# Conditioning loads of the last projection tiles moved to GpSimd's queue, value weights split ahead of the query rotation, five buffers for split queries and keys

## The chip, the core and the metric

The kernel runs on one core of a Trainium2 chip. The metric is the device time of one execution in microseconds; less is better. TensorE multiplies, VectorE (DVE) and ScalarE (ACT) work element by element, GpSimd (POOL) does some of that and starts transfers, and SyncE (SP) starts transfers only. ScalarE starts transfers too. Each engine takes its instructions in program order, and waits for others by semaphores.

## The reference

One encoder block on a sequence of 1024 positions with 1024 channels, all in float32:

```
ada = silu(c) @ w_ada + b_ada;  sh1, sc1, gt1, sh2, sc2, gt2 = split(ada, 6)
h = rms(x, g_pre_mix) * (1 + sc1) + sh1
q_lat, kv_lat, k_rope_raw, u, gate_cols = split(h @ w_in)       # 384, 256, 32, 512, 2048
branch_a = attention(rms(q_lat) @ w_uq, rms(kv_lat) @ w_uk, rms(kv_lat) @ w_uv, rotated parts) @ w_o
branch_b = a * sigmoid(g), where a, g = split(gelu(s5(u)) @ w_glu)   # s5: a state-space scan, both directions
mixed = (sigmoid(gate_a) * branch_a + sigmoid(gate_b) * branch_b) @ w_mix
x = x + gt1 * rms(mixed);  h = rms(x, g_pre_ffn) * (1 + sc2) + sh2
x = x + gt2 * rms((silu(h @ w_g) * (h @ w_up)) @ w_out)
```

`w_ada` is a 1024 x 6144 matrix that meets a single vector, so the conditioning is 48 column blocks of 128, each a row-wise dot product.

## The kernel before, in words

Channels lie on the partitions, positions in the free dimension, in two halves of 512. Every large product is done three times in a reduced format on split operands (high times high, high times low, low times high): `mm3`, lines 199 to 203. Weights come through `WStream` (line 150): SyncE loads a raw tile (two buffers), ScalarE casts its high part, VectorE subtracts the low part (three buffers of each). `get(ahead)` hands out a tile and splits as many as `ahead` beyond it, one by default; the loads of later raw tiles follow. The order of the list is: 26 tiles of `w_in`, three of `w_uq`, `w_uk`, `w_uv`, eight of `w_glu`, then the rest.

The stage around the change:

- **Projection tiles 10 to 25** (loop at line 950). `proj_tile` multiplies 48 large matmuls (two halves of eight blocks of three); between the halves and after them one step of the state-space part (until tile 22) and one step of a latent's norm is put in. ScalarE evacuates each half.
- **Norms of the latents** (`q_norm`, `kv_stats`, from tile 20 and 22): squares on ScalarE, their additions on VectorE (`lat_stats`, line 846), one-column sums on TensorE (line 245), a root in small VectorE steps, two diagonal tiles on VectorE, and `lat_apply` (line 862) spreads them by a matmul with ones (line 871), then scales and splits the latents.
- **Conditioning blocks 16 to 47** (`ada_load`, line 923, `ada_load2`, line 942, `ada_do`, line 933). A block of 512 KB, or two halves of 256 KB in buffers that the state-space part used (`er`, `ei`, `mr`, `mi`, `tz`, `r`), is multiplied by silu(c) and summed by VectorE. Two are loaded at tile 18, two each at tiles 20 to 22, four each at tiles 23 and 24, one in each gated-unit tile (`glu`, line 1118), and eight in the feed-forward part. At tile i the statements are: flush, `ada_do` (all live blocks), the next loads, a norm step. A load given to `later` goes on a list; `flush` starts all that is on it from ScalarE's queue:

```
    def later(dst, src):
        pending.append((dst, src))

    def flush(keep=0):
        while len(pending) > keep:
            A_.dma_start(*pending.pop(0))
```

- **Queries, keys, values.** Four tiles of the position-free queries (`uq_nope`, 18 large matmuls each), with the key and value latents' scaling between them; `uq_rope` (36 matmuls, then the rotation on VectorE out of four PSUM buffers, with the first Gelus of `y_chain` on ScalarE between its halves); then `uk_half` and `uv_tiles` by turns, six matmuls each, eight of both. `split_store` (line 1011) splits a query or key half in two and stores both parts to HBM by SyncE; its tiles are in the pool `sg`. PSUM has four buffers named `mm` and four named `s`; `uv_tiles` and every second half use `s`.
- Then eight gated-unit tiles, attention, the mixing product and the feed-forward part.

Of the kernel before, what the change touches and what calls it, by code (L numbers as in the profile page):

```python
# [33 lines left out]
KEEP0, ADA0, ADAN = 2, 18, 2  # L34
# [5 lines left out]
GLU_ADA, ATT_ADA = (1,) * NJ, (2,)  # L40
# [17 lines left out]
class Ops:  # L58
# [6 lines left out]
    def tt(self, o, a, b, op):  # L65
        return self.eng.tensor_tensor(o, a, b, op=op)  # L66
# [24 lines left out]
def _body(tc, a, out):  # L91
    nc = tc.nc
    V, A_, PE, G, SY = nc.vector, nc.scalar, nc.tensor, nc.gpsimd, nc.sync
# [6 lines left out]
    def pool(name, bufs=1, space=None, side=None, stack=None):  # L100
        kw = {}
        if space is not None:
            kw["space"] = space
        if side is not None:
            kw["side"] = side
        return (stack or es).enter_context(tc.tile_pool(name=name, bufs=bufs, **kw))
# [35 lines left out]
# [6 lines that stand above are left out]
# [153 lines left out]
    for kind, i, hs in units:  # L301
        if kind == "in":
            wl += [(a["wfi"][2 * i], KD * P), (a["wfi"][2 * i + 1], KD * P)]
        elif i < last or hs == (0,):
            c = 2 * FGROUPS[i] * P
            wl += [(a["wfo"][m, :, 2 * starts[i] * P:2 * starts[i] * P + c], c) for m in range(KD // 2)]
    win = WStream(wp, wl, D, (2, 3))
# [285 lines left out]
    nr = pool("nr", bufs=2, stack=q_es)  # L593
# [217 lines left out]
    def norm_step():  # L811
        for g in norms:
            next(g, None)

    def proj_tile(i, done):
        w = win.get()
        pss = []
        for h in range(2):
            ps = ps_mm()
            c = slice(h * HF, (h + 1) * HF)  # L820
            for k in range(KD):
                mm3(ps, w, hhi[k][:, c], hlo[k][:, c], k, k == 0, k == KD - 1)
            pss.append(ps)
            if i > 3:
                if h == 0:
                    s5_next()
                    norm_step()
        done(pss)
        if i > 3:
            s5_next()  # L830

    for i in range(4, 10):
        def done(ps, i=i):
            for h in range(2):
                t = ev.tile([P, HF], F32, name="ev", tag="ev")
                A_.copy(t, ps[h])
                A_.dma_start(pdram[i - 4, :, h * HF:(h + 1) * HF], t)
# [70 lines left out]
    def q_norm():  # L908
        raw = [load_rows(0), load_rows(1), load_halves(2, ("u", "u"), 3)]
        yield  # L910
        rc = yield from lat_stats(raw, lambda i: s5_half(f"t{i}"), ps_s5)
        yield from lat_apply(raw, rc, g_q, qhi, qlo, lambda i: s5_half(f"t{i}"), ps_s5)

    def kv_stats():
        raw = [load_halves(3 + i, (f"g{i}", f"g{i}"), 2) for i in range(2)]
        yield
        kv_rc.append((yield from lat_stats(raw, lambda i: s5_half(("vr", "vi", "z0")[i]), ps_s5)))
# [3 lines left out]
    ada_rest = list(range(16, 48))  # L921

    def ada_load(n, pl, tag, bufs=None, eng=G):
        for _ in range(min(n, len(ada_rest))):
            i = ada_rest.pop(0)
            t = pl.tile([P, D], F32, name=tag, tag=tag, bufs=bufs)
            if eng is None:
                later(t, a["wada"][i])
            else:
                eng.dma_start(t, a["wada"][i])  # L930
            ada_live.append((t, i))

    def ada_do(n=8):
        while ada_live and n:
            t, i = ada_live.pop(0)
            if isinstance(t, list):
                ada_reduce2(t, i)
            else:
                ada_reduce(None, t, i)
            n -= 1  # L940

    def ada_load2(tags):

        i = ada_rest.pop(0)
        t = [s5b.tile([P, 512], F32, name=n, tag=n, bufs=tags[2]) for n in tags[:2]]
        for x, c in zip(t, halves):
            later(x, a["wada"][i][:, c])
        ada_live.append((t, i))

    for i in range(10, 26):  # L950
        def done(ps, i=i):
            for h in range(2):
                t = ev.tile([P, HF], F32, name="ev", tag="ev")
                A_.activation(t, ps[h], AF.Sigmoid)
                A_.dma_start(gdram[i - 10, :, h * HF:(h + 1) * HF], t)
        proj_tile(i, done)
        flush()
        if ADA0 <= i < QN0:
            ada_do()
            if i < QN0 - 1:  # L960
                ada_load(ADAN, nr, "nr", None, None)
        if i >= QN0:
            ada_do()
            for tags, first in ADA_TAGS:
                if first <= i < 25:
                    ada_load2(tags)
            if i == QN0:
                norms.append(q_norm())
            if i == KN0:
                norms.append(kv_stats())  # L970
            norm_step()
# [12 lines left out]
    r_es = ExitStack()  # L984
# [4 lines left out]
    gp = pool("gp", bufs=2, side="right", stack=gp_es)  # L989
    yp = pool("y", side="right", stack=y_es)  # L990
    kvp = pool("kv", stack=r_es)
    rp = pool("rp", stack=r_es)
    sg = pool("sg", bufs=3, stack=r_es)
    csb = [rp.tile([P, S], F32, name=f"cs{i}") for i in range(2)]
    G.memset(vhi[:, :, :, 64:66].bitcast(F32), 1.0)
    G.memset(vlo[:, :, :, 64:66].bitcast(F32), 0.0)
# [69 lines left out]

    def uq_rope():

        w = win.get()
        pss = [dense_tile(w, i, 3, qhi, qlo) for i in range(2)]  # L1070
        qr = [qkd["qr"][e].rearrange("(h a r) s -> a h r s", a=2, r=16) for e in range(2)]
        yield
        prev = []
        for h, c in enumerate(halves):
            for i, op in enumerate((ALU.subtract, ALU.add)):
                ti = rp.tile([P, HF], F32, name="qra", tag="qra", bufs=3)
                u = rp.tile([P, HF], F32, name="qrb", tag="qrb")
                tt(ti, pss[i][h], csb[0][:, c], ALU.mult)
                tt(u, pss[1 - i][h], csb[1][:, c], ALU.mult)
                tt(ti, ti, u, op)  # L1080
                prev.append((ti, SCALE, [qr[e][i][:, :, c] for e in range(2)]))
                if len(prev) > 1:
                    split_store(*prev.pop(0))
            yield
        for p in prev:
            split_store(*p)
# [26 lines left out]
    def gb_load(m):  # L1113
        if m < KD:
            gbs[m] = gp.tile([P, S], F32, name="gb", tag="gb")
            later(gbs[m], gdram[m])

    def glu(m):

        w = win.get()  # L1120
        pa = dense_tile(w, 0, 4, yhi, ylo)
        pg = dense_tile(w, 1, 4, yhi, ylo)
        ada_do()
        ada_load(min(GLU_ADA[m], len(ada_rest) - 8), gp, "wada", 3, G if m else None)
        flush()
        gb = gbs.pop(m)
        sgm = gp.tile([P, S], F32, name="sgm", tag="sgm")
        for h, c in enumerate(halves):
            A_.activation(sgm[:, c], pg[h], AF.Sigmoid)
            tt(sgm[:, c], pa[h], sgm[:, c], ALU.mult)  # L1130
            tt(sgm[:, c], sgm[:, c], gb[:, c], ALU.mult)
        later(mbd[m], sgm)
        gb_load(m + 2)
# [3 lines left out]
    for i in range(4):  # L1137
        if i % 2 == 0:
            w = win.get()
# [13 lines left out]
    w = win.get()  # L1153
# [165 lines left out]
    for i in range(len(steps) + LAG):  # L1319
        if 0 <= i < len(steps):  # L1320
            h, kt = steps[i]
            if kt == 0 and h + 2 < NH:
                load_qk(h + 2)
            pt = scores(h, kt)
        j = i + LEAD
        if NJ <= j < len(steps):
            mh_, mt = steps[j]
            ps = mx_ps()
            max_tile(mh_, mt, [ps[:, c] for c in halves])
            V.reduce_max(mcol[mh_][:, mt:mt + 1], ps, axis=mybir.AxisListType.X)  # L1330
        if 0 <= i < len(steps):
            ptiles[i] = p_low(*pt)
        if NJ <= j < len(steps) and mt == NJ - 1:
            max_row(mh_)
        if i in ATT_ADA:
            ada_do(1)
            ada_load(min(1, len(ada_rest) - 8), gp, "wada", 3)
        if i == NJ:
            gp_es.close()
            op = pool("o", side="right", stack=o_es)  # L1340
            ohi += [op.tile([P, S], F32R, name=f"ohi{k}") for k in range(4)]
            olo += [op.tile([P, S], F32R, name=f"olo{k}") for k in range(4)]
        if NB <= i < len(steps):
            st = (i - NB) % (2 * NJ)
            if st == 0 and i >= 2 * NJ:
                norm_b(h // 2 - 1)
            if NC <= st < NC + 4 and i >= 2 * NJ:
                norm_c((i - NB) // (2 * NJ) - 1, st - NC)
        if i in (20, 28):
            win.split()  # L1350
            win.load()
        if i >= LAG:
            pv(*steps[i - LAG], ptiles.pop(i - LAG))
# [21 lines left out]
    with ExitStack() as m_es:  # L1375
# [39 lines left out]
        w = [win.get(), win.get()]  # L1415
# [5 lines left out]
        for m in range(KD):  # L1421
            if m >= 4 and m % 2 == 0:
                w = [win.get()]
# [238 lines left out]
    for u, (kind, i, hs) in enumerate(units):  # L1662
# [14 lines left out]
        if i < last:  # L1677
            for m in range(KD):
                if m % 2 == 0:
                    w = win.get()  # L1680
# [132 lines left out]
```

## Time and profile before

| | us |
|---|---|
| three runs | 1737.35, 1736.61, 1736.26 |
| median | 1736.61 |
| profiled execution | 1737.2 |
| its span, first to last instruction | 1735.4 |

| engine | busy us | share of the span |
|---|---|---|
| TensorE, matmuls | 1639.5 | 94% |
| TensorE, weight loads (beside the matmuls) | 1325.3 | 76% |
| VectorE | 976.7 | 56% |
| ScalarE | 553.1 | 32% |
| GpSimd | 147.9 | 9% |

The mean granted clock of TensorE is 0.968 of full speed. Starting transfers is not counted as busy. A queue of ScalarE or SyncE is written ACTq or SPq. A wait is put down to what came last before the waiting instruction began. Most vector helpers are recorded on lines 66 and 74, all large matmuls on lines 201 to 203, so the names of the tiles tell them apart: `mm` and `s` are PSUM, `whi` and `wlo` split weights, `sghi` and `sglo` split queries and keys, `er<-in_wada` a half of a conditioning block.

### The profile page before, as it was taken

The numbers are of one execution on the slowest core, as the hardware profiler recorded it, in microseconds if no ns is written. First come the engines' busy times: TensorE is split into PE (matmuls) and PEld (weight loads), VectorE is DVE, ScalarE is ACT, GpSimd is POOL, SyncE is SP. The second block draws the span as 40 slices with busy tenths as digits, with TensorE's granted clock in tenths as the row PEclk, the third lists the DMA queues.
The fourth block names the chain that finished last, engine by engine and source line by source line (L and its number), as shares of the span: only waits on it lengthen the run. The fifth ranks groups of instructions, "written<-read, shape, count | busy, mean of one in ns | idle before, by whom it ended". The sixth has DMA issues, their size and how long they took to land.

```text
span 1735.4 us, 19440 instructions
## 1 busy us (share of the span) xinstructions
PE 1639.5 (94%) x7486; PEld 1325.3 (76%) x7486; DVE 976.7 (56%) x1613; ACT 553.1 (32%) x743; POOL 147.9 (9%) x191
## 2 busy tenths in 40 slices
PE   7989999986869999999999999999999999999995
PEld 7868887875648867776777777888888888888875
DVE  4978898844574777885455565222322322323367
ACT  3242312222252147767233344321111121111243
POOL 0340000000031000000233220000000000000002
PEclk9899999987889999999999999999999999999998
DMA  6342333452878541420443252212211111111234
GB/s 260 121 119 96 111 102 96 132 171 93 277 233 265 153 126 34 98 44 13 153 133 128 79 200 94 99 58 72 71 55 52 61 38 48 60 32 46 83 119 148
DMA packets 92540, 189.67 MB, mean 109 GB/s; under 512 B 19992, under 2 KB 36504, under 8 KB 92448
## 3 DMA queue, kind: packets, MB, share of 16 engines
q1 hardware_dynamic: 57920, 120.62, 22.8%
q10 hardware_dynamic: 31424, 58.34, 9.7%
q0 software_dynamic: 3104, 9.47, 1.8%
q8 instruction: 59, 0.97, 0.2%
q14 instruction: 33, 0.27, 0.1%
HBM read 148.61 MB, written 39.78 MB: 109 GB/s over the span
## 4 chain that ended last, share of the span: by engine, by line
PE 69%; DVE 17%; DMA 5%; ACT 5%; issue 3%; ACTq 1%; SPq 0%; DVEq 0%; POOLq 0%
PE mm L203 17%; PE mm L202 17%; PE mm L201 17%; DVE t L66 4%; PE sc L1251 2%; PE sc L1252 2%; PE sc L1253 2%; DVE wlo L66 2%; PE pv L1277 1%; PE pv L1276 1%; PE pv L1278 1%; ACT whi L183 1%; PE mm L1390 1%; PE mx L1199 1%; PE s L245 1%
## 5 line engine op out<-in xcount | busy, mean ns | idle before, releaser
L202 PE MATMUL mm<-mh,whi 128*128 128x512 f32 x736 | 288.9, 393 | 4.9 <-DVE mh L74 3.1
L203 PE MATMUL mm<-mh,wlo 128*128 128x512 f32 x736 | 288.9, 393 | 2.2 <-DVE wlo L66 2.1
L201 PE MATMUL mm<-mh,whi 128*128 128x512 f32 x736 | 289.6, 394 | 0.3 <-ACT whi L183 0.3
L66 DVE TENSOR_TENSOR wlo<-wraw,whi 128x1024 fp32r<-128x1024 f32 (+1 forms) x128 | 155.9, 1235 | 77.9 <-ACT whi L183 77.9
L66 DVE TENSOR_TENSOR silu<-mm,silu 128x512 f32<-128x512 f32 x44 | 30.4, 692 | 277.1 <-PE mm L203 270.9
L183 ACT CAST whi<-wraw 128x1024 fp32r<-128x1024 f32 (+1 forms) x128 | 129.9, 1035 | 165.0 <-PE mm L202 137.0
L202 PEld LDWEIGHTS mm<-mh,whi 128*128 128x128 f32 x736 | 139.0, 189 | 38.1 <-DVE mh L74 6.9
L203 PEld LDWEIGHTS mm<-mh,wlo 128*128 128x128 f32 x736 | 139.1, 189 | 33.1 <-DVE wlo L66 4.3
L201 PEld LDWEIGHTS mm<-mh,whi 128*128 128x128 f32 x736 | 139.3, 189 | 30.8 <-ACT whi L183 0.9
L201 PE MATMUL mm<-hhi,whi 128*128 128x512 f32 x384 | 159.1, 414 | 1.2 <-ACT ev L600 1.2
L202 PE MATMUL mm<-hlo,whi 128*128 128x512 f32 x384 | 154.5, 402 | 3.9 <-DVE hlo L74 3.9
L203 PE MATMUL mm<-hhi,wlo 128*128 128x512 f32 x384 | 154.8, 403 | 0.0
L201 PE MATMUL mm<-fhi,whi 128*128 128x512 f32 x304 | 118.8, 391 | 0.0
L202 PE MATMUL mm<-flo,whi 128*128 128x512 f32 x304 | 118.5, 390 | 0.0
L203 PE MATMUL mm<-fhi,wlo 128*128 128x512 f32 x304 | 118.3, 389 | 0.0
L66 DVE TENSOR_TENSOR mr<-mm,mr 128x512 f32<-128x512 f32 (+1 forms) x88 | 56.3, 641 | 97.1 <-PE mm L203 97.0
L66 DVE TENSOR_TENSOR plo<-p,phi 128x1024 fp32r<-128x1024 f32 x64 | 78.3, 1224 | 38.6 <-ACT phi L1257 38.3
L1609 ACT CAST fhi<-silu 128x512 fp32r<-128x512 f32 x44 | 27.3, 620 | 220.6 <-DVE silu L66 220.6
L202 PEld LDWEIGHTS mm<-hlo,whi 128*128 128x128 f32 x384 | 74.4, 194 | 21.8 <-DVE hlo L74 4.8
L201 PEld LDWEIGHTS mm<-hhi,whi 128*128 128x128 f32 x384 | 74.7, 194 | 19.9 <-issue 2.1
L203 PEld LDWEIGHTS mm<-hhi,wlo 128*128 128x128 f32 x384 | 74.1, 193 | 18.1
L1256 ACT ACTIVATE p<-sc 128x1024 f32<-128x1024 f32 x64 | 65.7, 1026 | 63.2 <-PE sc L1253 63.2
(517 smaller groups left out, 2951.2 us busy)
## 6 DMA issues: line engine op xcount, KB each, us to landing
wraw<-in_wfi SPq DMA_DIRECT2D x58, 512.0 KB
wraw<-in_win SPq DMA_DIRECT2D x26, 512.0 KB
wraw<-in_wfo SPq DMA_DIRECT2D x20, 512.0 KB
gdram<-ev ACTq DMA_DIRECT2D x32, 256.0 KB
wada<-in_wada POOLq DMA_DIRECT2D x15, 512.0 KB, 5.3
wraw<-in_wmix SPq DMA_DIRECT2D x10, 512.0 KB
xT<-in_xT SPq DMA_DIRECT2D x8, 512.0 KB
pw<-in_wadk SPq DMA_DIRECT2D x8, 512.0 KB
```

The lines of the kernel that those rows point to most:

```text
L66: return self.eng.tensor_tensor(o, a, b, op=op)
L183: A_.copy(hi, t)
L201: PE.matmul(ps, whi[:, c], rhi, start=first, stop=False)
L202: PE.matmul(ps, whi[:, c], rlo, start=False, stop=False)
L203: PE.matmul(ps, wlo[:, c], rhi, start=False, stop=last)
L245: PE.matmul(ps[:, j:j + 1], src[:, j * P:(j + 1) * P], ones[:, 0:1], start=first and j == 0, stop=last and j == w - 1)
L1199: PE.matmul(pieces[j], qt["qhi"][b][0:96, t * P:(t + 1) * P], qt["khi"][b][0:96, halves[j]], start=True, stop=True)
L1251: PE.matmul(ps[:, c], kh[0:97, kc], qh[0:97, c], start=True, stop=False)
L1252: PE.matmul(ps[:, c], kh[0:96, kc], ql[0:96, c], start=False, stop=False)
L1253: PE.matmul(ps[:, c], kl[0:96, kc], qh[0:96, c], start=False, stop=True)
L1256: A_.activation(p, ps, AF.Exp)
L1609: A_.copy(fh[:, c], t)
```

## The change

Five edits. The two kinds of conditioning loads of the projection tiles are started by GpSimd at the place where they were put on ScalarE's list. The pool of split queries and keys has five buffers for each of its two tiles (2 KB a partition each). `uq_rope` asks the stream for two tiles ahead, so the value weights are cast and subtracted before its matmuls are written, and the stream's next loads move with them. The buffer for conditioning blocks in the gated-unit tiles and in attention (4 KB a partition) is one instead of three.

```diff
@@ ada_load2 @@
         for x, c in zip(t, halves):
-            later(x, a["wada"][i][:, c])
+            G.dma_start(x, a["wada"][i][:, c])
@@ projection tiles @@
             if i < QN0 - 1:
-                ada_load(ADAN, nr, "nr", None, None)
+                ada_load(ADAN, nr, "nr", None)
@@ pools @@
-    sg = pool("sg", bufs=3, stack=r_es)
+    sg = pool("sg", bufs=5, stack=r_es)
@@ uq_rope @@
-        w = win.get()
+        w = win.get(2)
@@ glu @@
-        ada_load(min(GLU_ADA[m], len(ada_rest) - 8), gp, "wada", 3, G if m else None)
+        ada_load(min(GLU_ADA[m], len(ada_rest) - 8), gp, "wada", 1, G if m else None)
@@ attention @@
-            ada_load(min(1, len(ada_rest) - 8), gp, "wada", 3)
+            ada_load(min(1, len(ada_rest) - 8), gp, "wada", 1)
```

## Rows read from the trace of the kernel before

**Rows 1.** Busy time by window: stretch, length, engines' busy time, clock, DMA share, GB/s.
```profile
361.89:441.34 79.45, 61.72 (x256) 49.40 (x253) 32.87 (x85) 18.58 (x30) 0.00 (x0) 0.81 0.41 134
441.34:521.17 79.83, 55.95 (x209) 42.60 (x208) 53.87 (x98) 34.03 (x55) 19.37 (x12) 0.83 0.75 252
521.17:1735.40 1214.23, 1180.94 (x5159) 949.25 (x5157) 586.77 (x784) 399.09 (x515) 91.98 (x83) 0.99 0.30 92
...
460.00:470.00 10.00, 10.00 (x31) 6.78 (x30) 2.43 (x4) 2.89 (x5) 0.00 (x0) 0.73 0.95 338
```

**Rows 2.** Timeline of TensorE: start us, us, engine, line, operation, tiles, shape.
```profile
367.59 0.95 PE L245 MATMUL s<-ones,t 128*128 128x1 f32 x8
372.74 1.87 PE L245 MATMUL s<-ones,t 128*128 128x1 f32 x8 [4.20 <-DVE t L66]
...
430.14 0.39 PE L201 MATMUL mm<-hhi,whi 128*128 128x512 f32 x1
...
430.84 0.39 PE L201 MATMUL mm<-hhi,whi 128*128 128x512 f32 x1
```

**Rows 3.** Chain of waits that ended last, 320 to 560 us: start, us, what.
```profile
386.52 5.00 DMA er<-in_wada
...
396.77 0.70 DVE t L66
...
397.61 3.38 PE s L871 x4
```

**Rows 4.** Waits of TensorE, 361 to 522 us: total us, times, longest us.
```profile
PE s L1101 <- ACT whi L183: 12.8, 1, 12.8
PE s L245 <- DVE vi L66: 7.0, 1, 7.0
PE s L871 <- DVE t L66: 6.5, 1, 6.5
PE mm L871 <- DVE gb L66: 4.7, 1, 4.7
PE s L245 <- DVE t L66: 4.2, 1, 4.2
PE mm L203 <- DVE wlo L66: 3.8, 2, 3.3
```

**Rows 5.** Timeline of VectorE: its five waits for conditioning loads, in brackets.
```profile
367.56 0.69 DVE L462 SCALAR_TENSOR_TENSOR er<-er,sil 128x512 f32<-128x512 f32 x1 [3.68 <-DMA er<-in_wada]
...
391.55 0.69 DVE L462 SCALAR_TENSOR_TENSOR er<-er,sil 128x512 f32<-128x512 f32 x1 [17.39 <-DMA er<-in_wada]
...
411.72 0.69 DVE L462 SCALAR_TENSOR_TENSOR er<-er,sil 128x512 f32<-128x512 f32 x1 [8.34 <-DMA er<-in_wada]
...
434.50 0.69 DVE L462 SCALAR_TENSOR_TENSOR er<-er,sil 128x512 f32<-128x512 f32 x1 [8.54 <-DMA er<-in_wada]
...
446.93 0.69 DVE L462 SCALAR_TENSOR_TENSOR er<-er,sil 128x512 f32<-128x512 f32 x1 [1.76 <-DMA er<-in_wada]
```

**Rows 6.** The tile wada: loads that GpSimd starts, issue in ns, landing.
```profile
L930 POOL DMA_DIRECT2D wada<-in_wada x15: 530/530/602, 526.0 to 1276.4; - x15
...
DMA to landing us min/median/max: 3.8/5.3/10.7
```

**Rows 7.** Waits of ScalarE and VectorE for stores, 361 to 522 us.
```profile
ACT sghi L1016 <- DMA qnd<-sghi: 10.4, 4, 8.0
...
DVE sglo L74 <- DMA qnd<-sglo: 9.2, 4, 6.6
```

**Rows 8.** Timeline of ScalarE and VectorE around the rotation.
```profile
482.11 0.68 DVE L66 TENSOR_TENSOR qra<-mm,cs 128x512 f32<-128x512 f32 x1
...
493.17 0.68 DVE L66 TENSOR_TENSOR qrb<-s,cs 128x512 f32<-128x512 f32 x1
...
495.17 1.98 ACT L183 CAST whi<-wraw 128x1024 fp32r<-128x1024 f32 x2
...
497.87 2.35 DVE L66 TENSOR_TENSOR wlo<-wraw,whi 128x1024 fp32r<-128x1024 f32 x2
```

## The prediction, on record before the kernel ran

> **What bounds the kernel now.** I cut the span into stretches first, with the view of busy time by window [rows 1]. Behind 521 us TensorE is busy 1180.9 of 1214.2 us at a granted clock of 0.99: nothing that the change touches can gain there. In the two stretches ahead of it, of 79.45 and 79.83 us, it is busy 61.7 and 56.0 us at clocks of 0.81 and 0.83. The first holds projection tiles 22 to 25; the second the query, key and value projections up to the first gated-unit tile. How much is lost in them is counted from the work. At the full clock three 512-column matmuls follow each other in 0.70 us, 0.233 each [rows 2]. The first stretch holds 192 of these (44.8 us); 32 one-column sums at 0.95 us for eight (3.8); four spreads, 1.7 at full clock, since they took 3.38 at half [rows 2, 3]; and 24 small matmuls, which I estimate at 0.12 each like the sums (2.9). That is 53.2 us, so 26.2 are lost. The second holds 204 large matmuls and four spreads, 49.2 us; 30.6 are lost. Together 56.9 us: no more than that can come back.
>
> The waits of TensorE name the places [rows 4]: 4.2, 6.5 and 7.0 us in front of the latents' sums and spreads in tiles 22 to 24, then 3.3, 4.7 and 12.8. What they don't show is the clock afterwards: eight sums take 0.95 us before the wait of 4.2 and 1.87 behind it, so the granted clock fell from 2.4 to 1.2 GHz after that idling [rows 2]; the matmuls behind each long wait pay it too.
>
> All of the first five waits end on VectorE, so I asked what VectorE waited for [rows 5]: five times for a load of conditioning weights (`er<-in_wada`), 3.7, 17.4, 8.3, 8.5 and 1.8 us, 39.7 in all. The chain of waits shows how this reaches TensorE [rows 3]: a load started at 386.5 by ScalarE's queue, 5.0 us to its landing, the reductions, the root, the diagonal at 396.8, and the spread at 397.6 that TensorE had waited 6.5 us for. The load wasn't slow, it started late: `ada_load2` only puts it on a list, `flush` starts it one whole tile afterwards, and the next statement, `ada_do`, makes VectorE wait for it, with the norm's steps queued behind.
>
> **The change, part by part.** *Loads on GpSimd's queue* (30 transfers, lines 947 and 961). They now start when their buffer is free, which is when `ada_do` of the same tile has read it, and are wanted a tile later. GpSimd has nothing to do in the first stretch (0.00 busy [rows 1]). Its loads of 512 KB took 530 to 602 ns to issue and 3.8 to 10.7 us to land, median 5.3 [rows 6]; these are half as large, and I take 5.3. A pair of tiles' reductions is 4 x 0.69 us [rows 5] and small steps, 3.3 us. Then, tile by tile:
> - Tile 22, the wait of 4.2: VectorE's 3.7 us for the load go, its reductions stay in front of the last additions; 0.8 of the wait is left. With the half clock behind it (some 3 us) 6.5 back.
> - Tile 23, the spread: the loads land near 371, while VectorE now stands idle until 391; the diagonal is ready at about 379, TensorE comes at 384. All 6.5 us go, and 1.7 of half clock.
> - Tile 24, the sums: the reductions follow the first squares, the last additions end about when TensorE's first half does. 7.0 and some 4 of half clock go.
>
> That is nearly all of the first stretch, 25.5 of 26.2 us: tile 25 ends at 415.8 instead of 441.3. From TensorE's new middle of tile 24 (396.7) VectorE has 21.8 us of work: one split, eight half-wide steps, two rounds of four tiles' reductions (6.6 each), a root and the split of the first query weights. It ends at 418.5, if the eight loads of tile 24, started from 403 to 409 as their buffers come free, land in time; with 10.7 us each VectorE would end 3 us later, with 3.8 as reckoned. The split that cost 3.3 us is done by 412. The diagonal for the key and value latents is there at 422.2, two query tiles after 415.8 TensorE asks for it at 424.2: the 4.7 go too, with 2 us of slack.
>
> *Five buffers instead of three.* ScalarE and VectorE waited 10.4 and 9.2 us for stores of split queries [rows 7]. TensorE was busy beside most of it, but the scaled key latents, the key weights' split and so the rotation stood behind. VectorE's work from 418.5 to the rotation is 19 half-wide steps of 0.69 and four splits of at most 1.17 [rows 8], 17.8 us, so 436.3. TensorE needs 108 matmuls and the spreads from 415.8, 26.9 us, to 442.7, and hands over the rotation's first half at 440.6. Here transfers press: 9.9 MB (latents 1.0, weights 1.4, tables and rotary keys 1.5, stores 4.0, scan output 2.0, from the tiles' sizes) start at about 412.5, and at the 338 GB/s of 460 to 470 us [rows 1] they take 29.3 us, to 441.8. I add 4 us for this and let the rotation start at 444.6; the ends are 0 and 10.
>
> *Value weights split early.* One cast of 0.99 us on ScalarE and one subtraction of 1.17 on VectorE [rows 8] move in front of the rotation; they are counted above. A wait comes with it: ScalarE's cast now needs the load of these weights, started when the third query weights are split (about 424.5), at about 436, 11.5 us later. The nearest landings are 3.8 to 10.7 us, so I charge nothing; behind a late one would queue ScalarE's Gelu, the rotation's splits and all evacuations. What it buys: the rotation runs from 482.1 to its last read of PSUM at 493.85, 11.7 us [rows 8], and TensorE idled through it for 12.8. Now it can go on with three key halves and two value tiles, five units of six matmuls, 7.0 us, until PSUM gives no more room: the third value tile reuses a buffer of the rotation. So TensorE works from 442.7 to 449.7, waits until 456.3 (6.6), then has eleven units (15.4), 2 us of half clock and 1.5 until the evacuations, queued behind the rotation, catch up: the first gated-unit tile starts at 475.2 instead of 521.2.
>
> *One conditioning buffer instead of three in the gated units.* Each load follows, in the program, the reduction that frees the buffer, and is read a tile later. GpSimd waits a little longer; behind it in its queue stand memsets of a row that attention reads some 80 us later. Nothing. The total of SBUF stays: 8 KB a partition more for the splits, 8 KB less here.
>
> Sum: 46.0 us less. Against the profiled execution (1737.2 us with its span of 1735.4) that is 1691.2; the median of the runs stands 0.6 below that execution. I predict 1691.
>
> **The rivals.**
> - *Transfers bind.* If the 9.9 MB run at the 252 GB/s of the stretch [rows 1], they take 39 us; the rotation starts 10 us later than TensorE could, and with more half clock some 12 come on top of the forecast: 1703. For it: two stores had ScalarE and VectorE waiting 8.0 and 6.6 us at a stretch. Against: fewer loads share this stretch now.
> - *GpSimd starts loads slowly beside VectorE.* If each of the last eight waits out one reduction of 0.69 us, VectorE ends 5.5 us later, TensorE waits 3.5 for the diagonal and runs 3 us more at half clock: 1698. Against: issues of 530 to 602 ns. By the Trainium skill ("SBUF — State Buffer", section "SBUF: two separate sides") a transfer started on GpSimd can stand still while VectorE holds a port in a two-port mode, and the other queues are to be preferred; no row here shows such a load held up.
> - *The queue makes no difference.* If only issue time counted, the gain is what the chain spends on issues: some 12 of about 0.5 us, as on GpSimd [rows 6]: 1731. By the Trainium skill ("DMA: Bandwidth & Descriptors", section "SWDGE vs HWDGE vs iDMA") starting transfers from several engines saves no more than the issuing engine's time. Against: VectorE idle for 17.4 us in front of a load that took 5.0 [rows 3, 5].
> - *It doesn't do what it says.* The loads wait on GpSimd for buffers that come free as late as ScalarE's list was flushed: 1735. Against: `er` and `ei` are read for the last time by the same tile's reductions.
> - *Slower.* A load starts only after the reductions, so a landing time T is hidden only up to the 12 us or so between two of them. Beyond, VectorE waits T-12 in each of five tiles; as bad as before at T=20 (5 x 8 = 40), and at 25 it costs 25 us more with none of the later gain: 1757. For it: half-size loads on a second queue beside the first; against: no landing over 10.7.
>
> **How the numbers follow.** Forecast 0.62, between 1680 (all 56.9 us back) and 1699; transfers bind 0.17; slow starts 0.10; queue makes no difference 0.04; no effect 0.04; slower 0.03. The range that leaves out little more than the last cases is 1679 to 1708. Repeated runs of this kernel agree within 0.06%; I call anything within 0.2% (3.5 us) the same. Faster: the first four, 0.93; the same 0.04; slower 0.03.
>
> **What would show it.** In the profile after: no VectorE wait on `in_wada` in tiles 21 to 25 over 2 us; the waits of 4.2, 6.5 and 7.0 us gone and a granted clock of 0.97 or more up to the query projection; TensorE at the first query matmul by 418; one wait of some 7 us at a value matmul, not at its first; the first gated-unit matmul near 475. It is wrong if VectorE's waits return with GpSimd's loads as the releaser, if ScalarE waits for the value weights in front of the rotation, or if later stretches, equally long now, change by more than 3 us.

## Result: 2.55% less time, and the profile after

Over four runs each, on the same chip, the changed kernel took 1693.18 us (median; 1690.66 to 1694.62) and the kernel before 1736.98. The ratio is 0.9745, with a 95% interval of 0.9728 to 0.9762. The prediction was 1691, with a range of 1679 to 1708. The profiled execution took 1692.5 us, its span 1690.4, and the mean granted clock was 0.982. One run of one kernel further down took 2681 us at a granted clock of 0.56, and the figures given for that kernel leave it out.

The windows of the changed kernel, cut at the same places of the program as those of before [rows 1] (tile 22's first matmul, the first query matmul, the first gated-unit matmul; columns as there):

```profile
363.62:416.81 53.19, 53.01 (x258) 43.24 (x253) 38.63 (x110) 18.44 (x30) 12.89 (x24) 1.00 0.70 228
416.81:473.46 56.65, 50.51 (x209) 40.01 (x208) 44.12 (x66) 31.41 (x50) 16.35 (x11) 0.94 0.90 291
473.46:1690.40 1216.94, 1181.42 (x5159) 949.75 (x5157) 590.51 (x790) 400.94 (x520) 94.93 (x85) 0.98 0.30 92
```

The first stretch shrank from 79.5 to 53.2 us and the clock in it rose from 0.81 to 1.00: TensorE is busy in all of it. The second shrank from 79.8 to 56.7, at 0.94 instead of 0.83, although more bytes a second moved (291 GB/s for 252). The third kept its work. GpSimd's 12.89 us in the first stretch are the starts of 24 loads, 0.54 each: on GpSimd, unlike the other queues, the view counts starts as busy.

The waits of TensorE in the same part, 300 to 520 us (total us, times, longest):

```profile
PE s L1101 <- DVE qra L66: 5.4, 1, 5.4
PE s L759 <- DMA tz<-kdram: 1.1, 1, 1.1
PE mm L201 <- DVE sglo L74: 0.7, 2, 0.5
PE s L245 <- DVE t L66: 0.2, 1, 0.2
```

Of the waits of 7.0, 6.5, 4.7, 4.2 and 3.3 us [rows 4] one is left, at 0.2; the wait of 12.8 for the value weights has become one of 5.4 for the rotation's last read of PSUM. No VectorE wait on `er<-in_wada` is left [rows 5]. TensorE's timeline shows what became of the half clock at the sums and spreads [rows 2, 3]:

```profile
369.32 0.95 PE L245 MATMUL s<-ones,t 128*128 128x1 f32 x8
370.45 1.05 PE L245 MATMUL s<-ones,t 128*128 128x1 f32 x8 [0.18 <-DVE t L66]
...
385.31 1.88 PE L871 MATMUL s<-t,ones 128*128 128x512 f32 x4
...
398.23 0.95 PE L245 MATMUL s<-ones,vr 128*128 128x1 f32 x8
```

The second eight sums take 1.05 us instead of 1.87, and the four spreads 1.88 instead of 3.38.

Who waits for the loads now? The view of the tile `er` in the changed kernel (what ended the idle time in front of its instructions, us and times; who waited for it; then landing times, least, median, most):

```profile
  DVE er L462: 39.3, 8
  DVE t L66: 26.9, 2
...
  POOL er L947: 66.1, 10
...
DMA to landing us min/median/max: 2.9/3.8/5.9
```

There is still a wait, but GpSimd has it, 66.1 us in front of ten loads, and for the buffers instead of the data: 39.3 us for the reductions that free them, 26.9 for the state-space part's last reads. Nothing that TensorE needs at that time stands behind GpSimd's queue.

### The profile page after: what moved, and what is told of

It reads as the page before. It is cut to its first block, busy times and chain, and to the rows that moved or that the text cites. A ratio compares the mean times of both kernels' runs of the same rounds, so it can differ in the third digit from the quotient of the medians.

```text
span 1690.4 us, 19479 instructions
## 1 busy us (share of the span) xinstructions
PE 1626.0 (96%) x7486; PEld 1316.5 (78%) x7486; DVE 976.2 (58%) x1613; ACT 552.3 (33%) x743; POOL 164.2 (10%) x221
## 4 chain that ended last, share of the span: by engine, by line
PE 71%; DVE 16%; DMA 5%; ACT 4%; issue 3%; SPq 0%; ACTq 0%; DVEq 0%; POOLq 0%
PE mm L203 18%; PE mm L201 18%; PE mm L202 18%; DVE t L66 3%; DVE wlo L66 2%; PE sc L1251 2%; PE sc L1252 2%; PE sc L1253 2%; PE pv L1277 1%; PE pv L1276 1%; PE pv L1278 1%; DMA mxd<-mneg 1%; PE mx L1199 1%; ACT whi L183 1%; DVE mr L66 1%
## 5 line engine op out<-in xcount | busy, mean ns | idle before, releaser
L66 DVE TENSOR_TENSOR plo<-p,phi 128x1024 fp32r<-128x1024 f32 x64 | 78.3, 1224 | 39.3 <-ACT phi L1257 38.9
L203 PEld LDWEIGHTS mm<-hhi,wlo 128*128 128x128 f32 x384 | 73.2, 191 | 17.8
```

What stands on the lines that cost most here:

```text
L203: PE.matmul(ps, wlo[:, c], rhi, start=False, stop=last)
```

## Experiments

Ratios are to runs of the kernel before on the same chip; its medians were 1734.62, 1733.91 and 1734.86 us in the three sets. The changed kernel, run again in the second and third set, had 1687.84 and 1687.13 us, below the 1693.18 of the result and below what I expected of it (1690 to 1695, then 1688 to 1692); so I compare within a set. My theory at the start was the prediction's: the loads came late because the list held them back a whole tile.

**Both kinds of loads alone.** The kernel before with the edits of lines 947 and 961 and nothing else.

> The kernel before with the loads on GpSimd's queue and nothing else. Theory (VectorE's waits for late conditioning loads hold TensorE, the two other edits only shorten the rotation's stage): the waits of 4.2, 6.5, 7.0, 3.3 and 4.7 us and the half clock behind them go, the wait of 12.8 us at the first value matmul stays: 34 to 38 us less, 1699 to 1703 us. Rival (the three edits give about a third each): about 1722 us.

Measured: 1704.37 us, ratio 0.9826 (0.9812 to 0.9841), so 30.3 us less. Some two thirds of the whole gain is the loads', a little less than the 34 to 38 us that I expected. The waits are mostly as expected: those of 4.2, 6.5, 7.0, 3.3 and 4.7 us are gone but for 0.2, and the one at the first value matmul stays at 11.9; but one of 3.3 is new, at the first key matmul (448.03), and the view names no cause for it.

**Only the queue.** The loads stay on the list and come out of `flush` a tile later, but GpSimd starts them (`e` is `G` for the conditioning loads, else `A_`):

```diff
-            A_.dma_start(*pending.pop(0))
+            d, x, e = pending.pop(0)
+            e.dma_start(d, x)
```

> The kernel before, in which the conditioning loads stay on the list and are started by the same flush a tile late, but from GpSimd's queue instead of ScalarE's. Theory (the place in the program decides, not the queue): within 4 us of the kernel before, 1733 to 1740 us, and VectorE still waits over 30 us for in_wada. Rival (ScalarE's queue was the slow one): about 1700 us.

Measured: 1705.54 us, 0.9834 (0.9819 to 0.9848). My theory is refuted: the list and the tile of delay cost nothing here. GpSimd's timeline in this kernel, whose lines are numbered one higher from there on:

```profile
366.13 0.54 POOL L148 DMA_DIRECT2D er<-in_wada  x1 [9.37 <-DVE er L463]
...
372.55 0.54 POOL L148 DMA_DIRECT2D er<-in_wada  x1 [3.79 <-DVE er L463]
...
391.83 0.54 POOL L148 DMA_DIRECT2D er<-in_wada  x1 [16.66 <-DVE er L463]
```

Each start waits for one thing, the reduction that frees its buffer. In the changed kernel, where the statement stands a tile earlier, the same starts come at the same times:

```profile
366.35 0.54 POOL L947 DMA_DIRECT2D er<-in_wada  x1 [9.37 <-DVE er L462]
...
372.77 0.54 POOL L947 DMA_DIRECT2D er<-in_wada  x1 [3.79 <-DVE er L462]
...
390.50 0.54 POOL L947 DMA_DIRECT2D er<-in_wada  x1 [15.10 <-DVE er L462]
```

GpSimd has no other work there and runs ahead of the program's other engines to its next load, wherever that is written. ScalarE, in the kernel before, can't; its timeline around the late load of [rows 3]:

```profile
373.42 0.33 ACTq L955 DMA_DIRECT2D gdram<-ev  x1
382.86 0.60 ACT L954 ACTIVATE ev<-mm 128x512 f32<-128x512 f32 x1 [9.47 <-PE mm L203]
...
385.54 0.59 ACT L761 COPY ev<-s 128x512 f32<-128x512 f32 x1 [2.08 <-PE s L759]
386.15 0.33 ACTq L762 DMA_DIRECT2D ydram<-ev  x1
386.52 0.44 ACTq L147 DMA_DIRECT2D er<-in_wada  x1
```

The load stands behind the evacuations of a tile (`ev`), and these wait 9.5 and 2.1 us for TensorE's results. It is the third load of `er`, and its buffer had been free since the reduction that began at 367.56 [rows 5]; GpSimd, with only the queue changed, starts the same load at 366.13. What is behind an evacuation in an engine's queue starts when TensorE is done with that tile.

**Only the place.** The loads are written where the changed kernel has them, but on ScalarE's queue:

```diff
-            later(x, a["wada"][i][:, c])
+            A_.dma_start(x, a["wada"][i][:, c])
...
-                ada_load(ADAN, nr, "nr", None, None)
+                ada_load(ADAN, nr, "nr", None, A_)
```

> The kernel before, in which the loads are started at the new place but by ScalarE. Theory (place decides; but ScalarE now stands still until VectorE has read the buffer, in front of the squares and casts behind it): most of the gain, 1703 to 1713 us, with ScalarE waiting for VectorE's reductions. Rival one (GpSimd's queue is what counts): no gain, about 1737 us. Rival two (an idle queue isn't needed): the same as with GpSimd, 1699 to 1703 us.

Measured: 1705.89 us, 0.9842 (0.9824 to 0.9859). This is within the theory's span, but it overlaps with the two kernels above, so the whole time shows no cost of ScalarE's queue beyond noise. The trace does. From tile 22 to the first query matmul, first with both kinds of loads alone, on GpSimd's queue, then here:

```profile
363.58:418.32 54.74, 54.57 (x259) 44.39 (x253) 38.61 (x110) 18.44 (x30) 12.85 (x24) 0.97 0.67 224
```

```profile
361.69:426.04 64.35, 59.30 (x260) 48.23 (x254) 39.52 (x112) 18.43 (x30) 0.00 (x0) 0.89 0.57 187
```

So 9.6 us of this stretch's loss remain (7.3 up to the first gated-unit matmul). TensorE's waits, 300 to 520 us, and ScalarE's timeline show where:

```profile
PE s L245 <- DVE vi L66: 3.0, 1, 3.0
...
PE s L245 <- DVE t L66: 2.0, 1, 2.0
```

```profile
400.75 1.14 ACT L883 CAST qhi<-nr 128x512 fp32r<-128x512 f32 x2 [4.29 <-DMA er<-in_wada]
```

The waits were 7.0 and 4.2 [rows 4]; with GpSimd 0.2 is left of both. What stands in ScalarE's queue ahead of that cast are eight starts of loads, from 396.92 to 400.71; behind it come the last squares of the key latents, and their sums are what TensorE waits 3.0 us for. Of the 7.3 us the whole time shows 1.5 against both kinds of loads alone. One thing that gives some back is at the end: from VectorE's last addition to the end of the span it is 3.9 us in all four profiles without these loads on GpSimd's queue, this one among them, and 5.8 to 6.2 in all ten with them. The rest is no more than what the other stretches differ by from profile to profile.

So in the whole time queue and place stand in for each other: either gives some 29 us, both give 30. It took both, a place a tile late and a queue full of evacuations, to make VectorE wait for a load.

**Early value weights alone, and everything but them.** `win.get(2)` in the kernel before; then the changed kernel with `win.get()`.

> The kernel before with the value weights split early and nothing else. Theory: TensorE can do five units of six matmuls (7 us) inside its wait of 12.8 us, less what the earlier split costs the rotation: 5 to 8 us less, 1729 to 1732 us, and a wait of 5 to 7 us appears at the third value tile. Rival (the load of these weights comes late and the rotation waits for it): no gain or up to 4 us slower, 1737 to 1741 us.

Measured: 1727.09 us, 0.9955 (0.9939 to 0.9972): 7.5 less. The wait at the third value tile is there, 5.4 us.

> The changed kernel without the early split of the value weights. Theory: TensorE idles through the rotation again at the first value matmul, five units (7 us) and some half clock more: 8 to 11 us slower than the changed kernel, 1701 to 1704 us. Rival (with the loads early this wait is short anyway): the same, 1693 us.

Measured: 1695.31 us, 0.9774 (0.9751 to 0.9796), against 1687.84, 0.9734 (0.9721 to 0.9747), for the changed kernel in the same set: 7.5 more, a little under what I expected (the two intervals don't overlap). Its largest wait of TensorE is the old one, at nearly its old length:

```profile
PE s L1101 <- ACT whi L183: 12.2, 1, 12.2
```

The edit is worth the same with the other edits and without.

**Five buffers: everything but them, and them alone.** The changed kernel with `bufs=3` and three conditioning buffers again; then the kernel before with that edit alone.

> The changed kernel with three buffers for split queries and keys (and three for conditioning blocks) again. Theory: in the shorter stretch the stores are under more pressure, VectorE and ScalarE wait some 5 to 10 us for them and the rotation starts 4 to 8 us later: 1697 to 1702 us. Rival (the rotation waits for TensorE's matmuls, not for the stores): the same, 1693 us.

Measured: 1692.34 us, 0.9758 (0.9742 to 0.9774), 4.5 more than the changed kernel; the two intervals overlap a little, but in the trace the rotation starts 4.4 us later (446.85 for 442.48 in the same set). The waits for stores are back, ScalarE's and VectorE's from 363 to 500 us:

```profile
ACT sghi L1016 <- DMA qnd<-sghi: 10.3, 3, 7.6
```

```profile
DVE sglo L74 <- DMA qnd<-sglo: 10.7, 2, 8.3
```

With five buffers VectorE's is 2.9 and ScalarE's 2.7, for 9.2 and 10.4 before [rows 7].

> The kernel before with only the five buffers for split queries (and one conditioning buffer instead of three in the gated units). My theory: they shorten the waits for stores in front of the rotation, but while the diagonal of the key and value latents comes late (TensorE's wait of 4.7 us) and the conditioning loads still hold VectorE, at most a little of that reaches the end: 1731 to 1734 (0 to 3 us less). Rival: buffers and loads are worth the same in any company; with the loads in place the buffers gave 4.5 us and, with the early value weights as well, so here too: 1729.

Measured: 1728.97 us, 0.9967 (0.9956 to 0.9977), 5.9 less. I was wrong: I had thought the late diagonal would hide this. The rotation starts at 478.45 instead of 482.11 [rows 8] and the first gated-unit matmul is 3.2 us earlier. The rest of the 5.9 isn't placed: in this trace the part behind that matmul is shorter by 2.9 us, with nothing of the edit in sight there but the single conditioning buffer. But this is within the scatter: up to VectorE's last addition that part is 1207.5 us long here and 1210.3 in the kernel before, and the changed kernel alone has 1211.1, 1207.2 and 1208.8 in its three profiles.

The three edits alone give 30.3, 7.5 and 5.9, in sum 43.7; together they gave 43.8 us in the result's set, 46.1 and 47.7 in the second and third. They about add up, which fits that each takes a different wait out of one path.

**What holds the rotation.** In the changed kernel TensorE still waits 5.4 us for the rotation. VectorE's timeline there, and GpSimd's:

```profile
443.95 0.68 DVE L66 TENSOR_TENSOR qra<-mm,cs 128x512 f32<-128x512 f32 x1
...
447.19 2.31 DVE L66 TENSOR_TENSOR qra<-qra,qrb 128x512 f32<-128x512 f32 x1
449.43 2.84 DVE L74 SCALAR_TENSOR_TENSOR sglo<-qra,sghi 128x512 fp32r<-128x512 f32 x1
...
455.31 0.68 DVE L66 TENSOR_TENSOR qrb<-s,cs 128x512 f32<-128x512 f32 x1
```

```profile
446.54 5.18 POOL L1041 TENSOR_TENSOR ylo<-nr,yhi 128x1024 fp32r<-128x1024 f32 x2 [24.70 <-ACT yhi L1036]
```

Two steps of the same kind that take 0.69 us elsewhere take 2.3 and 2.8 while GpSimd subtracts `ylo`. So I moved the four subtractions to VectorE, one step later:

```diff
+        low = []
         for k, r in enumerate(raw):
+            if k > 1:
+                tt(*low.pop(0))
...
+            low.append((ylo[k], t, yhi[k].bitcast(F32), ALU.subtract))
             yield
-            gt(ylo[k], t, yhi[k].bitcast(F32), ALU.subtract)
+        for x in low:
+            tt(*x)
+            yield
```

> The changed kernel, with the low parts of the scan output subtracted by VectorE behind the rotation instead of GpSimd beside it. Theory (three of the rotation's VectorE steps take 2.31, 2.84 and 3.48 us instead of 0.69, 0.69 and 1.3 because GpSimd's subtractions run beside them): the rotation's last read of PSUM comes some 4 us earlier, TensorE's wait of 5.4 us at the third value tile shrinks to about 1: 4 to 6 us faster than the changed kernel, about 1688 us. Rival (VectorE's four subtractions of 1.23 us cost as much as they save): the same, 1693 us.

Measured: 1697.67 us, 0.979 (0.9777 to 0.9804), 9.8 longer than the changed kernel. The mechanism held: inside the rotation every step takes 0.68 or 0.69, and TensorE's wait for `qra` is 0.5. But the stretching went elsewhere. VectorE, GpSimd and ScalarE in this kernel:

```profile
437.90 1.80 DVE L74 SCALAR_TENSOR_TENSOR nr<-nr,vecs,sgm 128x512 f32<-128x512 f32 x1
439.62 2.88 DVE L66 TENSOR_TENSOR kvlo<-nr,kvhi 128x512 fp32r<-128x512 f32 x1
442.43 2.83 DVE L74 SCALAR_TENSOR_TENSOR nr<-nr,vecs,sgm 128x512 f32<-128x512 f32 x1
...
449.17 0.68 DVE L66 TENSOR_TENSOR qra<-mm,cs 128x512 f32<-128x512 f32 x1
```

```profile
436.75 2.39 POOL L1047 TENSOR_TENSOR kt<-kr,cs 32x1024 f32<-32x1024 f32 x1 [15.09 <-DVE kr L70]
439.22 2.73 POOL L1047 TENSOR_TENSOR kr<-kr,cs 32x1024 f32<-32x1024 f32 x1
442.03 2.68 POOL L1047 TENSOR_TENSOR kr<-kr,kt 32x1024 f32<-32x1024 f32 x1
```

```profile
459.93 1.06 ACT L1038 ACTIVATE nr<-ylo 128x1024 f32<-128x1024 f32 x1 [3.63 <-DVE ylo L66]
```

With GpSimd's queue empty, the rotary keys' steps, which had waited behind the subtractions until 468, ran at 437 to 445, beside the key latents' scaling: the rotation started at 449.2. And the third Gelu now waits for a subtraction behind the rotation, with the evacuations queued after it. This is about half of the loss: from tile 22 to the first gated-unit matmul it is 5.1 us more than the changed kernel of the same set (115.25 for 110.15). Behind that matmul the trace has another 5.0, 1.1 of them a wait of TensorE for the last subtraction; the rest isn't placed and is about as large as the scatter there.

The next kernel avoids both: the first two subtractions on VectorE, in their old place, the last two on GpSimd.

> The changed kernel with the low parts of the first two scan outputs subtracted on VectorE, the other two on GpSimd as before, so that the rotary keys' steps stay behind them in GpSimd's queue. My theory: GpSimd's two subtractions stretch two VectorE steps of the rotation by 2.0 and 2.15 us; on VectorE one of them falls inside the rotation, at 1.22 us, so the rotation's last read of PSUM comes some 2 to 3 us earlier, TensorE's wait at the third value tile falls from 5.7 to about 3, and the key latents' scaling is not touched: 2 to 4 us less than the changed kernel. Rival: what stretches the steps is something else than GpSimd's work (ScalarE's reads, transfers): the steps stay at 2.7 us, VectorE has 2.4 us more to do, and the time is 1 to 3 us longer.

Measured: 1686.69 us, 0.9724 (0.9703 to 0.9744); the changed kernel of the same set had 1687.13, 0.9734 (0.9716 to 0.9751). No difference can be measured. From the rotation's start to the first gated-unit matmul this kernel takes 28.0 us, the changed kernel 29.5, 29.8 and 29.6 in three profiles, so some 1.6 is there. TensorE's waits:

```profile
PE s L1101 <- DVE qra L66: 2.8, 1, 2.8
PE mm L201 <- DVE sglo L74: 1.9, 2, 1.7
```

The wait for the rotation fell as expected, from 5.4 to 2.8, and part of it came back at an evacuation: VectorE's second subtraction, behind the rotation, runs beside the third, on GpSimd, and takes 3.42 us instead of 1.22:

```profile
453.88 3.42 DVE L66 TENSOR_TENSOR ylo<-nr,yhi 128x1024 fp32r<-128x1024 f32 x1
```

The last kernel asks, besides, for one more key half ahead of the third value tile.

```diff
             uk_half(m, w, h)
-            next(uv)
+            if 2 * m + h != 2:
+                next(uv)
...
+    next(uv)
```

> As the kernel with the first two low parts on VectorE, and one more key half (six matmuls, 1.4 us) asked for ahead of the third value tile. My theory: the two PSUM buffers of the rotation's first half are free at about 446, so this unit runs in TensorE's gap and the wait falls by another 1.4 us, to about 1.5; with less half clock behind it 3 to 6 us less than the changed kernel. Rival: the unit's own buffer waits for an evacuation that stands behind the rotation, so that it can't run earlier than the value tile: the same time as without the new order, or a unit's wait more.

Measured: 1690.94 us, 0.9748 (0.973 to 0.9765): not the 3 to 6 us less that I expected but 3.8 more than the changed kernel, with intervals that overlap. The unit ran in the gap, as the theory had it, and the wait at the third value tile is 1.1; but the next key half found no free buffer. TensorE and ScalarE:

```profile
452.41 0.50 PE L1101 MATMUL s<-whi,kvhi 128*128 128x512 f32 x1 [1.13 <-DVE qra L66]
...
459.96 0.80 PE L201 MATMUL mm<-kvhi,whi 128*128 128x512 f32 x1 [5.90 <-DVE sglo L74]
```

```profile
460.27 0.37 ACT L1107 CAST vhi<-s 128x256 fp32r<-128x256 f32 x1 [4.21 <-DVE vlo L66]
```

The sum of the two waits is 7.0, more than the 4.7 without the new order, and the stretch from the rotation's start takes 31.7 us. What bounds this place is not the order in which TensorE asks but when VectorE gets to the evacuations. No version clearly beat the changed kernel.

## Why the prediction was right

Taken step by step, predicted and measured:

| step | predicted | measured |
|---|---|---|
| tile 22, wait at the second sums | 0.8 us left | 0.2 |
| length of the first stretch | 53.9 us | 53.2 (363.62 to 416.81) |
| length of the second stretch | 59.4 us | 56.7 |
| VectorE's last reduction ends | 418.5 | 419.5 |
| diagonal for key and value latents | 422.2 | 423.6, no wait at the spread (425.0) |
| rotation starts | 444.6 | 443.95 |
| its last read of PSUM | 456.3 | 456.0 |
| wait at the third value tile | 6.6 us | 5.4 |
| first gated-unit matmul | 475.2 | 473.46 |
| less time at that point | 46.0 us | 47.7 |
| less time in the whole execution | 46.0 us | 44.7 |

*The loads.* The sizes held: landings of 2.9 to 5.9 us for `er`, median 3.8, and at most 6.0 for the others, against the 5.3 taken from larger ones [rows 6]. Tile 22 itself started 1.7 us later than before, 1.1 of it a wait on `tz<-kdram` that no edit touches; in the fourteen profiles it starts between 359.2 and 364.4. The cause was half right. "It started late" is shown; that it did so because `flush` starts it "one whole tile afterwards" is refuted by the kernel that keeps the list and changes the queue. The right sentence is that it stood, a tile late, in ScalarE's queue behind evacuations that wait for TensorE. The forecast came out all the same, since the edit takes the loads off both; that it did so with a wrong reason for the delay is luck.

*The rival that the queue makes no difference* had the price 1731. The kernel with only the queue changed refutes it at 1705.5. With the early place, ScalarE's and GpSimd's queue differ by 1.5 us in the whole time, less than the measurement can tell, though by 7.3 in the trace up to the first gated-unit matmul; with the late place, by 29 us in the whole time. The Trainium skill's sentence behind that rival ("DMA: Bandwidth & Descriptors", section "SWDGE vs HWDGE vs iDMA"), that starting transfers from several engines saves no more than the issuing engine's time, agrees with the first pair, where ScalarE's eight starts in a row take 3.8 us ahead of its cast; it doesn't speak of the second, where the engine's queue waits for TensorE ahead of the load.

*The rival that GpSimd starts loads slowly beside VectorE* is refuted: every half-size load was issued in 0.54 us, as the rows above show, and the longest landing was 6.0. What the two engines do to each other showed in another place: steps with two SBUF inputs took 2.3 and 2.8 us instead of 0.69 beside GpSimd's subtractions, while those with an input in PSUM kept their length. The steps `qra<-s,cs` don't show this, since GpSimd is idle beside them (451.72 to 456.96), but an evacuation beside the last subtraction of the changed kernel does:

```profile
466.67 2.40 POOL L1041 TENSOR_TENSOR ylo<-nr,yhi 128x1024 fp32r<-128x1024 f32 x1 [7.11 <-ACT yhi L1036]
```

```profile
467.12 0.69 DVE L74 SCALAR_TENSOR_TENSOR sglo<-mm,sghi 128x512 fp32r<-128x512 f32 x1 [2.11 <-ACT sghi L1016]
```

The Trainium skill ("SBUF — State Buffer", section "SBUF: two separate sides") has the rule for it: a VectorE operation with two SBUF inputs and a GpSimd operation that reads SBUF shut each other out for a whole instruction. The trace agrees: in the kernel with two subtractions on VectorE, the one of 3.42 us ends 1.1 us after GpSimd's of 453.60 to 456.20 has ended, close to the 1.22 that it takes alone.

*Transfers bind* did not come true: the stretch moved 291 GB/s instead of 252, and the 4 us that I added for them covered the delay. They weren't all transfers: TensorE handed over the rotation's first half at about 441, and VectorE, with 17.0 us of work for the 17.8 that I had reckoned, came to it at 443.95 after 7.3 us of waits, 2.9 for a store and 4.3 for ScalarE.

*Five buffers.* The prediction gave them no price of their own, only the path behind the stores; alone they are worth 4 to 8 us by the interval.

*The rival that the change is slower* has a price that its own terms don't give: 25 us more than 1737 is 1762, not 1757. Nothing else rests on it.

*What the forecast didn't hold.* It counted the last stretch as unchanged; it is 2.7 us longer (1216.9 for 1214.2), just under the 3 us that the prediction named as a sign of being wrong. VectorE's last addition begins at 1684.51 instead of 1731.50, 47.0 earlier, so 0.7 of the 47.7 was lost on the way, within the scatter of that part. The span ends 5.9 us after it instead of 3.9. These two microseconds belong to the queue: all ten profiles with these loads on GpSimd's queue have 5.8 to 6.2 there, all four without them 3.9. It isn't the last output, which lands 2.8 us after the addition's start in both kernels; what GpSimd does between that and the end stays open. So the closeness of 44.7 to 46.0 is in part luck: from tile 22 to the first gated-unit matmul the change gave 49.4 us, 3.4 more than forecast, and the later start (1.7), the scatter (0.7) and the end (2.0), none of which it held, brought this down to 45.0 in the span.

## What to carry to other kernels

In these traces a transfer started when everything ahead of it in its engine's queue was done. Before weighing the cost of an issue, look at what stands in front of it: behind an evacuation it waited for TensorE, and an engine that is idle in that stretch, or a place a tile earlier, each gave nearly all of the gain alone. Look then at a stretch and not only at the whole time: the place alone left 7 us that the whole time hid. When an engine's work is taken away, look at what moves up in its queue: the steps that it had held back may now run beside something worse, as the rotary keys did.

## What the runs showed of the hardware

- GpSimd's steps on two SBUF tiles (subtractions of 128x1024, rotary steps of 32x1024) lengthened VectorE's steps with two SBUF inputs, 0.69 to 0.75 us alone, to between 1.8 and 2.9, and a 1024-wide one from 1.22 to 3.42. An evacuation with an input in PSUM took 0.69 beside a subtraction.
- GpSimd's transfers of 256 KB were issued in 0.54 us each beside a VectorE busy with reductions of two SBUF inputs, and landed after 2.9 to 6.0 us; ScalarE's in the kernel before that stand in its chain of waits took 3.2 to 7.0.
- With these loads on GpSimd's queue the program's end came 2.0 us later after the last addition (5.8 to 6.2 us in ten profiles) than without (3.9 in four).
